# Layer 0 to 1 of a hybrid encoder: weight blocks split by VectorE, normed rows transposed one row tile later, one key transpose moved, no copy of group A's reciprocals

## The chip, the cores and the metric

The kernel runs on one core of a Trainium2 chip. The core has a matrix engine (TensorE, "PE" in the profile; its weight loads are "PEld"), three engines for elementwise work (VectorE "DVE", ScalarE "ACT", GpSimd "POOL"), SyncE ("SP"), which issues the DMAs, an on-chip memory (SBUF) and a small accumulator memory that PE writes (PSUM). Each engine has its own instruction queue and works it off in order; semaphores tie the queues together. The metric is the device time of one execution in microseconds (us). Lower is better.

## The reference: what is computed

Two encoder layers over a sequence of 1024 tokens with 1024 features, in float32. Each layer normalises x, projects it, runs two groups of attention heads beside each other, gates their outputs, projects the result, normalises it again and adds it to x:

```python
for l in range(DEPTH):                       # DEPTH = 2
    h = rms_norm(x, pre_norm_g[l])
    proj = h @ w_in[l]                       # 1024 x 3328
    aq, ak, av, ag, bq, bk, bv, bg = jnp.split(proj, SPLIT_POINTS, axis=-1)
    ...
    oa = diff_attention(...)                 # softmax(q1 k1) - lam * softmax(q2 k2), 4 heads
    oa = rms_norm(oa, diff_subln_g[l]) * (1.0 - lam_init)
    ya = oa.reshape(bn, s_len, A_WIDTH) * jax.nn.silu(ag)
    q = apply_rope(rms_norm(bq, q_norm_g[l]), cos, sin)   # 8 heads
    k = apply_rope(rms_norm(bk, k_norm_g[l]), cos, sin)   # 2 heads
    ob = gqa_attention(q, k, bv)
    yb = ob * jax.nn.silu(bg)
    y = jnp.concatenate([ya, yb], axis=-1) @ w_out[l]
    x = x + rms_norm(y, post_norm_g[l])
```

## The kernel before

**Precision.** Every float32 operand of a matmul is split into two parts in the format fp32r: a rounded one ("hi") and the rest ("lo"). ScalarE makes hi by a copy, and VectorE or GpSimd makes lo by a subtraction. A product is three matmuls (`mm3`: hi hi, hi lo, lo hi), so one row tile of 128 tokens by 512 columns is 8 x 3 = 24 matmuls (`mm_tok`).

**Tiling.** The tokens are 8 row tiles of 128. A projection goes through chunks of weight columns. `tok_chunk` runs over row tiles: 24 matmuls into PSUM, then a `post` function that hands the result on, then `follow`, which runs deferred steps whose due time ("beat", one per 512 columns) has come, then the `side` steps, mostly weight conversions. Every row tile of x must be transposed before it can be multiplied: `prenorm_b` transposes 8 blocks of 128x128 on PE into two PSUM tiles named pT (four blocks each), and `split` writes hi (ScalarE) and lo (VectorE) into the transposed tiles hT. PSUM holds **two** pT buffers in all; queries and keys use the same two.

**Weights.** `w_steps` gives the loads and the conversions of a chunk in blocks of 128x1024 elements. `on_dve` lists the blocks whose lo part VectorE makes; GpSimd makes the others.

**Layer 0, queries.** In the first stage the key/value columns are projected for the 8 tiles. Each tile's keys are scaled, and transposed some steps later (`bkv_store`: one transpose, split, four DMAs). The keys of tile 6 are transposed by the entry at due time 5 of the query chunk's `queue`, those of tile 7 at the same beat, and each tile's queries (`bq_store`: four transposes) two beats after they are made.

**Attention.** `all_items` yields score tiles for both groups, and `tick` lays the steps of several of them beside one another: scores, row sums, exponentials, transposes, product with V. For group A, `combine` forms reciprocals of the two row sums with VectorE; one scales the second softmax map, the other is copied into `r0`, from which `norm` and `gate` scale the result on GpSimd.

**Layer 0 to 1.** The output projection runs in two halves of 512 columns. In the second half's loop over row tiles t, the instructions of four engines keep the written order. For each t the loop does the residual of tile t-1 on VectorE (the result is x for the next layer and goes to DRAM), the norm of an earlier tile (`pre_normed`, VectorE), the transposes of a still earlier one (`pre_transposed`), the squares for the norm (`pre_scale`, ScalarE), then the 24 matmuls, the square and the scaling of their result (`out_half`), `post_scale`, and the `hooks` of that t: conversions of the next layer's key/value weights (`kv_convs`, two blocks) and query weights (`q_convs`, four blocks), the rotary tables, and the next layer's lambdas. The steps left over, `ends`, are run by layer 1: two at once, the others at the beats of `DUES`, between the key/value tiles (half a beat each).

The scale of a row goes through GpSimd: VectorE forms the mean square, GpSimd raises it to the power -1/2 (`rpow`).

Of the kernel before, what the change touches and what calls it, by code (L numbers as in the profile page):

```python
# [20 lines left out]
NT = 8  # L21
# [11 lines left out]
DVE_OUT = (1, 3)  # L33
ENDING = (1, 2, 3, 4, 0, 5)
BIAS = 3
DUES = (0.5, 1.5)
QSIDE = lambda c: {0: c[:1], 1: c[1:]}
FD = 1
OUTORD = True
# [12 lines left out]
def hybrid_encoder(ctx, tc, x, rel_bias, pre_norm_g, w_in, diff_lambda, diff_subln_g,  # L52
# [250 lines left out]
    def layer(l, hT, ends, given):  # L303
# [145 lines left out]
        if l == 0:  # L449
# [76 lines left out]
            queue.append((1, last_kv))  # L526
            for t in lates:
                queue.append((t - NT + LT, lates[t]))
            queue.append((5, lambda: lates[NT - 2]()))
            w_aq, loads, convs = w_steps(wl, C_AQ, on_dve=(1, 3))  # L530
            tok_chunk(w_q, bq_post, side={0: loads[:2], 1: convs[:1], 2: convs[1:2] + loads[2:], 4: convs[2:3],
                                          5: convs[3:]})
# [102 lines left out]
        def a_items(q, K, T5, t, qi, aT, r0, out):  # L635
            bias = T5[:, 896 - P * t:896 - P * t + 1024]
            es = [None, None]
            sums = s_tile(2, "asum", 4)
            items = []
            for c in range(2):  # L640
                def scores(c=c, box=[]):
                    pS = ps_s()
                    for i in range(2):
                        x0 = qi * 512 + i * 256 + c * P
                        for kh in range(2):
                            n = slice(kh * 512, kh * 512 + 512)
                            pe.matmul(pS[:, n], q[:, x0:x0 + P], K[:, c, n], start=(i == 0), stop=(i == 1))
                    return pS

                def reduce(pS, c=c):  # L650
                    es[c] = e_tile()
                    m = s_tile()
                    dve.tensor_tensor_reduce(out=es[c], in0=pS, in1=bias, op0=ALU.add, op1=ALU.min,
                                             scale=1.0, scalar=3.0e38, accum_out=m)
                    return m

                def expo(pS, m, c=c):
                    act.activation(es[c], es[c], AF.Exp, bias=m, scale=-1.0, accum_out=sums[:, c:c + 1])
                    if c == 1:
                        after(CD, combine)  # L660
                items.append((scores, reduce, expo))

            def combine():
                rec = s_tile(2, "arec", 4)
                dve.reciprocal(rec, sums)
                cc = s_tile()
                dve.scalar_tensor_tensor(cc, sums[:, 0:1], neglam, rec[:, 1:2], ALU.mult, ALU.mult)
                dve.tensor_copy(r0[:, qi:qi + 1], rec[:, 0:1])
                a, b = es
                gps.tensor_scalar(b, b, cc, 0.0, ALU.mult, ALU.add)  # L670
                gps.tensor_tensor(a, a, b, ALU.add)

                def go():
                    return transpose_unit(a, aT, qi, None) + [lambda: parts.extend(out or [])]
                trans.append((now[0] + AD, go))
            return items

        def a_out(h, g, aT, r0):
            box = []

            def part(i):
                if i == 0:
                    box.append(ps_o())
                pO = box[0][:, 0:256]
                V = values[h]
                for k in (2 * i, 2 * i + 1):
                    pe.matmul(pO, V[:, 0, k, :], aT[0][:, k, :], start=(k == 0), stop=False)
                    pe.matmul(pO, V[:, 0, k, :], aT[1][:, k, :], start=False, stop=False)
                    pe.matmul(pO, V[:, 1, k, :], aT[0][:, k, :], start=False, stop=(k == NK - 1))
                if i == 3:  # L690
                    after(0, lambda: finish(box[0]))

            def finish(pO):
                oT = o_tile((P, 256))
                act.copy(oT, pO[:, 0:256])
                p4 = pO[:, 256:512].rearrange("p (q c) -> p q c", c=P)
                ms = s_tile(2, "oms", 3)
                yv = [ys[g * 2 + qi][:, h * P:(h + 1) * P] for qi in range(2)]

                def norm():  # L700
                    for qi in range(2):
                        pe.transpose(p4[:, qi, :], oT[:, qi * P:(qi + 1) * P], ident)
                    for qi in range(2):
                        act.activation(oT[:, :P], p4[:, qi, :], AF.Square, accum_out=ms[:, qi:qi + 1])
                    after(1, gate, True)

                def gate():
                    for qi in range(2):
                        dve.tensor_tensor(yv[qi], p4[:, qi, :], yv[qi], ALU.mult)
                    fr = s_tile(2, "ofr", 3)  # L710
                    gps.tensor_tensor(fr, r0, r0, ALU.mult)
                    gps.tensor_tensor(ms, ms, fr, ALU.mult)
                    gps.tensor_scalar(ms, ms, 1.0 / P, EPS, ALU.mult, ALU.add)
                    gps.tensor_tensor(ms, ms, mhalf[:, :2], ALU.pow)
                    gps.tensor_tensor(fr, ms, r0, ALU.mult)
                    for qi in range(2):
                        gps.tensor_scalar(yv[qi], yv[qi], fr[:, qi:qi + 1], 0.0, ALU.mult, ALU.add)
                after(1, norm)

            return [lambda i=i: part(i) for i in range(4)]  # L720
# [105 lines left out]
        def all_items():  # L826
            for h in range(4):
                KA, T5 = state["ak"]
                if h:
                    load_av(h)  # L830
                if h == 0:
                    state["bv"] = h_tile([P, 2, NT, P], F32R)
                    nc.sync.dma_start(f(state["bv"]), bv_d)
                if h == 2:
                    state["bk"] = load_bk(1)
                BK, BV = state["bk"], state["bv"]
                for g in range(4):
                    q = state["q"]

                    if (h, g) != (3, 3):  # L840
                        state["q"] = load_q(h + (g + 1) // 4, (g + 1) % 4)
                    else:
                        for fn in half_loads:
                            fn()
                    if g == 0 and 0 < h < 3:
                        state["ak"] = load_ak(h + 1)
                    aT = new_probs()
                    bT = [None, None]
                    r0 = s_tile(2, "r0", 4)
                    sr = s_tile(4, "sr", 4)  # L850
                    a_parts = a_out(h, g, aT, r0)
                    b_parts = b_out(h, g, BV, bT, sr)
                    yield from a_items(q, KA, T5, g * 2, 0, aT, r0, None)
                    for j in range(2):
                        bT[j] = new_probs()
                        for qi in range(2):
                            if j and qi and not (h or g):
                                load_av(0)
                                state["ak"] = load_ak(1)
                            yield from b_items(q, BK, j, qi, bT, sr, b_parts[j] if qi else None)  # L860
                        if j == 0:
                            yield from a_items(q, KA, T5, g * 2 + 1, 1, aT, r0, a_parts)
# [106 lines left out]
        def pre_transposed(t):  # L969
            prenorm_b(t, yn[t], hN[t // 4])  # L970
# [8 lines left out]
        w = load_w(w_out[l], 512)  # L979
        hN, xts, hooks, nxt = [], [None] * NT, {}, None  # L980
        if not last:
            n_kv, kv_loads, kv_convs = w_steps(w_in[l + 1], C_BK, 256)
            n_q, q_loads, q_convs = w_steps(w_in[l + 1], C_BQ, on_dve=(3,))
            for fn in kv_loads + q_loads[:2]:
                fn()
            box = []
            hooks = {0: kv_convs[:1], 1: kv_convs[1:] + [lambda: box.extend(load_tables(l + 1))],
                     2: q_convs[:1] + [lambda: box.append(load_gains(l + 1))],
                     3: q_convs[1:2] + [lambda: box.append(lambdas(l + 1))],
                     4: [lambda: box.append(box[3]()), lambda: fill_tables(box[0], box[1], box[2], 1, gps)],  # L990
                     5: [lambda: fill_tables(box[0], box[1], box[2], 0, gps)], 7: q_loads[2:]}
        everything = [nc.tensor, nc.vector, nc.scalar, nc.gpsimd]
        for t in range(NT):
            xts[t] = e_tile()
# [2 lines left out]
            if t >= 1:  # L997
                residual(t - 1)
            if not last:
                if t in (3, 7):  # L1000
                    hN.append(new_h(t // 4))
                if t >= 2:
                    pre_normed(t - 2)
                if t >= 3:
                    pre_transposed(t - 3)
                if t >= 1:
                    pre_scale(t - 1)
            if last and t == NT - 1:
# [10 lines left out]
        else:  # L1019
            nxt = n_kv, n_q, q_convs[2:], box[0], *box[4]  # L1020

            def seventh():
# [1 line left out]
                residual(7)  # L1024
                pre_scale(7)

            ends = [lambda: pre_transposed(5), seventh, lambda: (pre_transposed(6), pre_normed(7))[:0],
                    lambda: pre_transposed(7)]
        inorder[:] = []
        return hN, nxt, ends  # L1030

# [57 lines left out]
```

## Time and profile before

| what | us |
|---|---|
| median of 3 runs | 1470.03 (1468.3 to 1470.81) |
| the profiled execution | 1470.85 |
| its span, first to last instruction | 1469.0 |
| PE busy | 1432.3 |
| VectorE busy | 843.9 |
| ScalarE busy | 775.3 |
| GpSimd busy | 741.7 |

The profile comes from one execution. Its span is the time from the first to the last instruction; the execution's own time is 1.85 us longer. Names of tiles are printed without their numbers: pS, pO and pT are PSUM tiles (scores and projections, projections and outputs, transposes), h are transposed rows, raw weights, keys and values, w converted weights and attention weights, y row tiles and their queries and keys, e temporaries of 128x1024, s small columns, o temporaries. In a timeline a row holds start, duration, engine, line, operation, output<-input, shapes and count; in brackets stands the engine's idle time ahead of it and who ended it. All instructions show line 65, because a helper class issues them, so one tells them apart by tiles and shapes.

### The profile page before, as it was taken

What the parts mean: (1) busy time and instruction counts of PE and PEld (TensorE: products, weight loads), DVE (VectorE), ACT (ScalarE), POOL (GpSimd) and SP (SyncE); (2) the same over time, 40 slices, a digit from 0 to 9 for tenths busy, and PEclk for the clock granted to TensorE, in tenths of its full rate; (3) what the DMA queues carried; (4) which work ended last, traced back from release to release, by engine and by line L of the source; (5) the groups of instructions that cost most, each with busy time, mean ns of one, the idle gap of its engine ahead of it and who ended that gap; (6) DMA issues with size and microseconds to landing.
All of it is one profiled execution on the core that took longest, in us unless ns stands there. A gap on an engine that the chain in (4) does not pass through costs nothing.

```text
span 1469.0 us, 22474 instructions
## 1 busy us (share of the span) xinstructions
PE 1432.3 (97%) x8300; PEld 1251.7 (85%) x8300; DVE 843.9 (57%) x1657; ACT 775.3 (53%) x1508; POOL 741.7 (50%) x743
## 2 busy tenths in 40 slices
PE   6999999999999999999899999999999999999998
PEld 6877888888999999988788888888799999998887
DVE  7851110038888888852786511100588888888424
ACT  5322122138888888852342322121588888888321
POOL 3541222018888888852433431120388888888320
PEclk9999999999999999999999999999999999999999
DMA  6468822165424322041335673223644142310303
GB/s 218 122 171 207 273 95 52 29 188 153 107 66 112 88 71 81 2 144 58 133 110 129 159 200 121 86 51 105 177 118 105 49 125 66 94 59 32 113 29 129
DMA packets 110669, 162.45 MB, mean 111 GB/s; under 512 B 8408, under 2 KB 72408, under 8 KB 108256
## 3 DMA queue, kind: packets, MB, share of 16 engines
q1 hardware_dynamic: 110560, 161.02, 37.8%
q8 instruction: 65, 1.06, 0.3%
q14 instruction: 44, 0.36, 0.1%
HBM read 112.72 MB, written 52.46 MB: 112 GB/s over the span
## 4 chain that ended last, share of the span: by engine, by line
PE 86%; issue 5%; DVE 4%; POOL 2%; ACT 1%; DMA 1%; POOLq 0%; SPq 0%; DVEq 0%; ACTq 0%
PE pS L65 39%; PE pO L65 34%; PE pT L65 12%; DVE y L65 2%; POOL w L65 1%; DVE h L65 1%; ACT e L65 1%; POOL e L65 0%; DVE s L65 0%; ACT w L65 0%; DMA y<-in_x_dram 0%; POOL s L65 0%; DVE w L65 0%; DMA h<-in_w_out_dram 0%; DVE e L65 0%
## 5 line engine op out<-in xcount | busy, mean ns | idle before, releaser
L65 PE MATMUL pO<-w,h 128*128 128x256 f32 (+1 forms) x3592 | 656.1, 331 | 0.2
L65 PEld LDWEIGHTS pO<-w,h 128*128 128x128 f32 x3592 | 569.5, 190 | 82.5 <-POOL w L65 0.8
L65 PE MATMUL pS<-h,h 128*128 128x512 f32 x1024 | 294.6, 409 | 0.0
L65 POOL TENSOR_TENSOR w<-h,w 128x1024 fp32r<-128x1024 f32 x56 | 135.3, 2435 | 267.2 <-ACT w L65 264.8
L65 PE MATMUL pT<-identr,e 128*128 128x128 f32 x1536 | 200.8, 273 | 1.5 <-DVE w L65 1.2
L65 PEld LDWEIGHTS pS<-h,h 128*128 128x128 f32 x1024 | 174.8, 189 | 24.6 <-ACT e L65 0.4
L65 PE MATMUL pS<-w,h 128*128 128x512 f32 (+1 forms) x912 | 195.4, 371 | 0.0
L65 POOL TENSOR_SCALAR e<-e,s 128x1024 f32<-128x1024 f32 x64 | 71.9, 1124 | 229.8 <-DVE s L65 229.8
L65 DVE TENSOR_TENSOR w<-pT,w 128x512 fp32r<-128x512 f32 x256 | 169.8, 684 | 31.6 <-ACT w L65 31.5
L65 PEld LDWEIGHTS pS<-w,h 128*128 128x128 f32 x912 | 159.7, 191 | 27.8
L65 PEld LDWEIGHTS pT<-identr,e 128*128 128x128 f32 x1536 | 172.6, 140 | 6.0 <-DVE w L65 5.1
L65 PE MATMUL pS<-h,w 128*128 128x512 f32 x768 | 177.0, 391 | 0.0
L65 POOL TENSOR_TENSOR s<-s,mhalf 128x2 f32<-128x2 f32 (+2 forms) x96 | 80.4, 838 | 189.9 <-DVE s L65 184.3
L65 POOL TENSOR_TENSOR w<-e,w 128x512 fp32r<-128x512 f32 x128 | 168.7, 1318 | 10.4
L65 PEld LDWEIGHTS pS<-h,w 128*128 128x128 f32 x768 | 143.4, 188 | 30.5 <-issue 0.5
L65 ACT CAST w<-pT 128x512 fp32r<-128x512 f32 x256 | 143.8, 588 | 45.8 <-PE pT L65 43.0
L65 DVE TENSOR_REDUCE s<-pS 128x1 f32<-128x1024 f32 x128 | 156.1, 1219 | 16.1 <-PE pS L65 15.2
L65 ACT ACTIVATE e<-e,s 128x1024 f32<-128x1024 f32 x128 | 148.1, 1157 | 22.4 <-DVE s L65 21.7
L65 DVE CUSTOM_DVE_ANT_0 e<-pS,h 128x1024 f32<-128x1024 f32 x128 | 155.4, 1215 | 5.5 <-PE pS L65 4.9
L65 POOL TENSOR_TENSOR e<-e,e 128x1024 f32<-128x1024 f32 x64 | 153.2, 2393 | 5.3
L65 ACT ACTIVATE e<-pS,s 128x1024 f32<-128x1024 f32 x128 | 144.5, 1129 | 7.3 <-issue 5.8
L65 ACT ACTIVATE o<-pO 128x128 f32<-128x128 f32 (+2 forms) x97 | 37.0, 382 | 130.6 <-PE pO L65 120.0
(77 smaller groups left out, 1095.6 us busy)
## 6 DMA issues: line engine op xcount, KB each, us to landing
h<-in_w_in_dram SPq DMA_DIRECT2D x52, 512.0 KB, 4.9
h<-aq_d SPq DMA_DIRECT2D x64, 256.0 KB, 5.1
bq_d<-y SPq DMA_DIRECT2D x64, 128.0 KB, 2.6
aq_d<-e SPq DMA_DIRECT2D x32, 256.0 KB, 4.4
ak_d<-e SPq DMA_DIRECT2D x16, 512.0 KB, 4.6
h<-bq_d SPq DMA_DIRECT2D x32, 256.0 KB, 6.0
h<-ak_d SPq DMA_DIRECT2D x16, 512.0 KB, 7.8
av_d<-e SPq DMA_DIRECT2D x32, 256.0 KB, 2.5
```

The lines of the kernel that those rows point to most:

```text
L65: ins = fn(*args, **kw)
```

## The change

It has four parts.

1. *Weight blocks.* Both key/value blocks of layer 1 and the first query block get their lo part from VectorE, not GpSimd. The second query block stays with GpSimd, but its conversion goes from the hooks of tile 3 to those of tile 6.
2. *Transposes.* In the second half's loop, the transposes of tile t-4 are issued at t (before: t-3), from t = 4 on. The second set of transposed tiles (rows 4 to 7) is created in `ends`, no longer at t = 7. `ends` has one step more, and `DUES` one beat more.
3. *Key transpose.* The entry for the keys of tile 6 in layer 0's query chunk goes from due time 5 to 4.
4. *Reciprocals.* `r0` has four columns. The reciprocals of both sums are written straight to it, with a stride of two, and the copy of 128x1 goes. The readers use its first two columns.

```diff
-DUES = (0.5, 1.5)
+DUES = (0.5, 1.0, 2.0)
...
-            queue.append((5, lambda: lates[NT - 2]()))
+            queue.append((4, lambda: lates[NT - 2]()))
...
             def combine():
-                rec = s_tile(2, "arec", 4)
+                rec = r0[:, qi::2]
                 dve.reciprocal(rec, sums)
                 cc = s_tile()
                 dve.scalar_tensor_tensor(cc, sums[:, 0:1], neglam, rec[:, 1:2], ALU.mult, ALU.mult)
-                dve.tensor_copy(r0[:, qi:qi + 1], rec[:, 0:1])
...
-                    gps.tensor_tensor(fr, r0, r0, ALU.mult)
+                    gps.tensor_tensor(fr, r0[:, :2], r0[:, :2], ALU.mult)
...
-                    gps.tensor_tensor(fr, ms, r0, ALU.mult)
+                    gps.tensor_tensor(fr, ms, r0[:, :2], ALU.mult)
...
-                    r0 = s_tile(2, "r0", 4)
+                    r0 = s_tile(4, "r0", 4)
...
-            n_kv, kv_loads, kv_convs = w_steps(w_in[l + 1], C_BK, 256)
-            n_q, q_loads, q_convs = w_steps(w_in[l + 1], C_BQ, on_dve=(3,))
+            n_kv, kv_loads, kv_convs = w_steps(w_in[l + 1], C_BK, 256, on_dve=(0, 1))
+            n_q, q_loads, q_convs = w_steps(w_in[l + 1], C_BQ, on_dve=(0, 3))
...
-                     3: q_convs[1:2] + [lambda: box.append(lambdas(l + 1))],
+                     3: [lambda: box.append(lambdas(l + 1))],
...
-                     5: [lambda: fill_tables(box[0], box[1], box[2], 0, gps)], 7: q_loads[2:]}
+                     5: [lambda: fill_tables(box[0], box[1], box[2], 0, gps)], 6: q_convs[1:2], 7: q_loads[2:]}
...
-                if t in (3, 7):
-                    hN.append(new_h(t // 4))
+                if t == 4:
+                    hN.append(new_h(0))
                 if t >= 2:
                     pre_normed(t - 2)
-                if t >= 3:
-                    pre_transposed(t - 3)
+                if t >= 4:
+                    pre_transposed(t - 4)
...
-            ends = [lambda: pre_transposed(5), seventh, lambda: (pre_transposed(6), pre_normed(7))[:0],
-                    lambda: pre_transposed(7)]
+            ends = [lambda: (hN.append(new_h(1)), pre_transposed(4)), seventh, lambda: pre_transposed(5),
+                    lambda: (pre_transposed(6), pre_normed(7))[:0], lambda: pre_transposed(7)]
```

On PE, in layer 0's query chunk, the order before (y_647 and y_714 are the keys of tiles 6 and 7, y_702 and y_766 queries of two tiles; of each group of 24 matmuls the first row is shown):

```order
L65 MATMUL pT_880<-identr,y_702 128x128 x4
L65 MATMUL pS_892<-w_324,h_84 128x512
...
L65 MATMUL pT_928<-identr,y_647 128x128
L65 MATMUL pT_937<-identr,y_714 128x128
L65 MATMUL pT_947<-identr,y_766 128x128 x4
L65 MATMUL pO_963<-w_324,h_84 128x512
```

And of the change:

```order
L65 MATMUL pT_879<-identr,y_647 128x128
L65 MATMUL pT_889<-identr,y_702 128x128 x4
L65 MATMUL pS_901<-w_324,h_84 128x512
...
L65 MATMUL pT_937<-identr,y_714 128x128
L65 MATMUL pT_947<-identr,y_766 128x128 x4
L65 MATMUL pO_963<-w_324,h_84 128x512
```

The transpose of tile 6's keys moved ahead of the earlier query group, so that each gap between matmul groups holds two pT tiles.

On VectorE, in the second half of layer 0's output projection, from the PSUM read of tile 0 to the norm of row 0, before (y_6920 and y_6965 are the rows of tiles 0 and 1, e_7234 and e_7273 their x, e_6878 the next layer's gain, s small scales):

```order
L65 TENSOR_TENSOR y_6920<-pO_7236,e_6876 128x512
L65 TENSOR_TENSOR s_7265<-s_6922,s_7262 128x1
L65 TENSOR_SCALAR s_7265<-s_7265 128x1
L65 SCALAR_TENSOR_TENSOR y_6920<-y_6920,s_7265,e_7234 128x1024
L65 TENSOR_SCALAR s_7279<-s_7277 128x1
L65 TENSOR_TENSOR y_6965<-pO_7282,e_6876 128x512
L65 TENSOR_TENSOR s_7311<-s_6967,s_7308 128x1
L65 TENSOR_SCALAR s_7311<-s_7311 128x1
L65 SCALAR_TENSOR_TENSOR y_6965<-y_6965,s_7311,e_7273 128x1024
L65 SCALAR_TENSOR_TENSOR y_6920<-y_6920,s_7279,e_6878 128x1024
```

And of the change (rows y_6856 and y_6901; w_7206 the lo part of the key/value weights):

```order
L65 TENSOR_TENSOR y_6856<-pO_7172,e_6812 128x512
L65 TENSOR_TENSOR s_7201<-s_6858,s_7198 128x1
L65 TENSOR_SCALAR s_7201<-s_7201 128x1
L65 TENSOR_TENSOR w_7206<-h_7164,w_7205 128x1024
L65 SCALAR_TENSOR_TENSOR y_6856<-y_6856,s_7201,e_7170 128x1024
L65 TENSOR_SCALAR s_7215<-s_7213 128x1
L65 TENSOR_TENSOR y_6901<-pO_7218,e_6812 128x512
L65 TENSOR_TENSOR s_7247<-s_6903,s_7244 128x1
L65 TENSOR_SCALAR s_7247<-s_7247 128x1
L65 TENSOR_TENSOR w_7206<-h_7164,w_7205 128x1024
L65 SCALAR_TENSOR_TENSOR y_6901<-y_6901,s_7247,e_7209 128x1024
L65 SCALAR_TENSOR_TENSOR y_6856<-y_6856,s_7215,e_6814 128x1024
```

The two subtractions of the key/value weights now stand between the small scales of a tile and its residual; on GpSimd they are gone.

On PE, from tile 2 of that half on, before (the first row of each matmul group; y_6920, y_6965 are rows 0 and 1):

```order
L65 MATMUL pO_7330<-w_7212,h_6880 128x512
...
L65 MATMUL pT_7382<-identr,y_6920 128x128 x4
L65 MATMUL pT_7389<-identr,y_6920 128x128 x4
L65 MATMUL pO_7401<-w_7212,h_6925 128x512
...
L65 MATMUL pT_7443<-identr,y_6965 128x128 x4
L65 MATMUL pT_7450<-identr,y_6965 128x128 x4
L65 MATMUL pO_7462<-w_7212,h_6970 128x512
```

And of the change (y_6856, y_6901 are rows 0 and 1):

```order
L65 MATMUL pO_7266<-w_7148,h_6816 128x512
...
L65 MATMUL pO_7319<-w_7148,h_6861 128x512
...
L65 MATMUL pT_7363<-identr,y_6856 128x128 x4
L65 MATMUL pT_7370<-identr,y_6856 128x128 x4
L65 MATMUL pO_7382<-w_7148,h_6906 128x512
...
L65 MATMUL pT_7435<-identr,y_6901 128x128 x4
L65 MATMUL pT_7442<-identr,y_6901 128x128 x4
```

Tile 3's matmuls now stand between those of tile 2 and the transposes of row 0, and all later transposes follow one tile later: row 4 stands ahead of the first key/value tile of layer 1, row 5 behind the first, row 6 behind the second and row 7 behind the fourth. Before, row 5 stood ahead of the first, row 6 behind the first and row 7 behind the third.

## The prediction

> **What bounds the kernel now.** I read the busy time by stage first, then the TensorE (PE) timeline around each place where PE was not busy, then the engine that it waited for.
>
> ```profile
> span 1469.0 us, 22474 instructions
> 136.00:312.00 176.00, 176.00 (x777) 145.80 (x777) 21.31 (x23) 33.32 (x43) 28.90 (x12) 1.00 0.43 136
> 340.00:627.00 287.00, 286.96 (x2028) 265.76 (x2027) 250.82 (x507) 251.52 (x507) 239.83 (x272) 1.00 0.30 80
> 690.00:766.00 76.00, 69.64 (x360) 58.16 (x359) 54.59 (x85) 29.26 (x60) 28.40 (x27) 0.96 0.35 122
> ```
>
> The columns are the stretch, its length, then busy time of PE, PE's weight loads, VectorE (DVE), ScalarE (ACT) and GpSimd (POOL), PE's granted clock, DMA share and GB/s. In layer 0's later projections (136 to 312) PE is busy all the time, in its attention (340 to 627) 286.96 of 287.00 us: nothing off PE can be worth time there. The stage between the layers (690 to 766) has 6.4 us without a matmul and a clock of 0.96. So only places where PE waits matter. The change touches two of them.
>
> The first is in layer 0's query chunk:
>
> ```profile
> 70.82 0.60 PE L65 MATMUL pT<-identr,y 128*128 128x128 f32 x4
> 71.18 5.74 PE L65 MATMUL pS<-w,h 128*128 128x512 f32 x24
> 76.75 0.38 PE L65 MATMUL pT<-identr,y 128*128 128x128 f32 x2
> 80.58 0.66 PE L65 MATMUL pT<-identr,y 128*128 128x128 f32 x4 [3.45 <-DVE y L65]
> 80.99 7.31 PE L65 MATMUL pO<-w,h 128*128 128x512 f32 x24
> 88.14 0.60 PE L65 MATMUL pT<-identr,y 128*128 128x128 f32 x4
> ```
>
> Two key transposes (tiles 6 and 7) run at 76.75, and the query tile's four behind them wait 3.45 us for VectorE. Only two pT buffers exist: the third transpose group needs the first one's buffer back. VectorE gives it back late:
>
> ```profile
> 74.31 0.68 DVE L65 TENSOR_TENSOR y<-pT,y 128x512 fp32r<-128x512 f32 x1
> 80.24 0.48 DVE L65 TENSOR_TENSOR y<-pT,y 128x128 fp32r<-128x128 f32 x2
> ```
>
> The split of both key tiles runs at 80.24, behind a whole query tile's rotary work. PE goes on 0.3 us later, and its next 24 matmuls take 7.31 us instead of 5.74.
>
> The second place is the end of layer 0's output projection:
>
> ```profile
> 677.97 32.90 PE L65 MATMUL pO<-w,h 128*128 128x512 f32 x144
> 713.98 1.94 PE L65 MATMUL pT<-identr,y 128*128 128x128 f32 x8 [3.11 <-DVE y L65]
> 715.57 7.80 PE L65 MATMUL pO<-w,h 128*128 128x512 f32 x24
> ...
> 738.84 1.25 PE L65 MATMUL pT<-identr,y 128*128 128x128 f32 x8 [1.04 <-DVE h L65]
> 739.85 5.75 PE L65 MATMUL pO<-w,h 128*128 128x512 f32 x24
> 746.16 1.26 PE L65 MATMUL pT<-identr,y 128*128 128x128 f32 x8 [0.56 <-DVE h L65]
> ...
> 757.17 1.06 PE L65 MATMUL pT<-identr,y 128*128 128x128 f32 x8 [0.55 <-DVE y L65]
> 757.99 3.11 PE L65 MATMUL pO<-w,h 128*128 128x256 f32 x24
> 760.94 3.04 PE L65 MATMUL pS<-w,h 128*128 128x256 f32 x24
> 763.85 1.06 PE L65 MATMUL pT<-identr,y 128*128 128x128 f32 x8
> 764.67 3.12 PE L65 MATMUL pO<-w,h 128*128 128x256 f32 x24
> 767.63 2.68 PE L65 MATMUL pS<-w,h 128*128 128x512 f32 x11
> ```
>
> Six row tiles end at 710.87 (713.98 less 3.11), so a tile takes 5.45. From start to start a key/value tile takes 2.94 and eight transposes 0.8. From 710.87 to the first query matmul at 767.63 PE has to do five tiles (27.25), eight groups of transposes (6.4) and four key/value tiles (11.75): 45.4 us. It took 56.8. **11.4 us** are waits and slow matmuls (7.80 against 5.75), and no more can be won there.
>
> **The change, part by part.**
>
> *Key transpose of tile 6 one query tile earlier.* It now stands at 70.82, in front of the query's four. The row at 70.82 shows no wait, so a buffer is free there, and the other was split a turn earlier. The groups then run as key 6, query, key 7, query, and the second pair takes the buffers of the first, whose splits VectorE does at about 74.3 to 75.1 (the row at 74.31, with the key's 0.2 ahead of it). At 76.75 neither group waits. PE does the same transposes (0.11 us each), so the matmuls of 80.99 start at 77.3 and, without a wait ahead of them, take 5.6 to the next transposes: 82.9 instead of 88.14, **5.3 us less**. The bounds are 0 (the wait comes back elsewhere) and 5.3. On SP the key's four stores go ahead of three query stores. What stands behind them, the next weight loads, is paced by conversions that move with PE. With PE busy 176.00 of 176.00 us in the stretch that follows, nothing there gives the time back; I take all of 5.3.
>
> *Blocks converted by VectorE.* Three GpSimd subtractions of 128x1024 (two key/value blocks, one query block) become VectorE's, and one query block's goes from after tile 3 to after tile 6.
>
> ```profile
> 700.67 1.04 ACT L65 CAST w<-h 128x1024 fp32r<-128x1024 f32 x1
> 700.81 0.69 DVE L65 TENSOR_TENSOR y<-pO,e 128x512 f32<-128x512 f32 x1 [4.69 <-ACT o L65]
> 702.35 2.40 POOL L65 TENSOR_TENSOR w<-h,w 128x1024 fp32r<-128x1024 f32 x1
> 702.42 3.42 DVE L65 SCALAR_TENSOR_TENSOR y<-y,s,e 128x1024 f32<-128x1024 f32 x1 [0.67 <-POOL s L65]
> 709.24 4.59 DVE L65 SCALAR_TENSOR_TENSOR y<-y,s,e 128x1024 f32<-128x1024 f32 x2 [0.67 <-POOL s L65]
> 735.71 2.47 DVE L65 SCALAR_TENSOR_TENSOR y<-y,s,e 128x1024 f32<-128x1024 f32 x2
> 766.52 1.21 DVE L65 TENSOR_TENSOR w<-h,w 128x1024 fp32r<-128x1024 f32 x1
> ```
>
> VectorE's residual took 3.42 while GpSimd's 2.40 ran, two of its kind 4.59 beside another, and 2.47 (1.2 each) undisturbed: a GpSimd block costs VectorE about 2.1 us. Done by VectorE it costs 1.21. So each moved block shortens VectorE's queue by 0.9 us, although a conversion now stands ahead of the residual: residual 0 ends at 701.7 (ACT's cast) + 1.2 + 1.2 = 704.2 instead of 705.8, and the normed row 0 is there by about 711.5 instead of 713.8. What queues behind the conversion on VectorE are the residual, ScalarE's square of it and the next PSUM read. All end earlier than before.
>
> *Transposes one row tile later.* Tile 3's matmuls now fill the 3.11 us: they run from 710.87 to 716.3, row 0 has been ready for nearly 5 us, and the slow clock behind the wait has no cause. Next late is VectorE's split of each transposed tile, which gives the two pT buffers back:
>
> ```profile
> 731.58 0.67 DVE L65 TENSOR_TENSOR y<-pO,e 128x512 f32<-128x512 f32 x1
> 740.96 4.54 DVE L65 SCALAR_TENSOR_TENSOR y<-y,s,e 128x1024 f32<-128x1024 f32 x2 [0.66 <-POOL s L65]
> 755.75 2.47 DVE L65 SCALAR_TENSOR_TENSOR y<-y,s,e 128x1024 f32<-128x1024 f32 x2
> 761.23 1.29 DVE L65 TENSOR_TENSOR h<-pT,h 128x512 fp32r<-128x512 f32 x2 [0.20 <-ACT h L65]
> ```
>
> 1. Tile 4 ends at 717.1 + 5.45 = 722.55, transposes of row 1 follow with 0.1 wait at most, tile 5 ends at 728.85.
> 2. Behind tile 4, VectorE has the next layer's lambdas. From its PSUM read (731.58) to the transposes that need the split at that iteration's end (738.84) it took 7.26. Now the read starts 0.8 after tile 4 (as 700.81 after 700.0), at 723.35, so row 2 is transposed at 730.6: **1.75 wait**. Tile 6 runs from 731.6 to 737.05.
> 3. The next turn of VectorE, with table filling on GpSimd beside it (4.54 for two), took 7.32 (738.84 to 746.16). Row 3 comes at 738.0: **0.95 wait**; tile 7 ends at 744.5.
> 4. The late query block on GpSimd makes the following turn as long: row 4 at 745.3, **0.8 wait**. The block's buffer becomes part of the second h tile; read to the end at about 743 (begun at 740.3, 2.40 long), it is needed at 746.
> 5. Row 5 comes between the first two key/value tiles without a wait (749.3). Row 6 needs row 5's split. Its chain held 755.75 + 2.47 to 761.23 + 0.65, or 3.65; the residual of tile 7 now ends at about 750.8 (row 3's split to 746.0, the PSUM read and two scales 1.1, row 4's split 1.3, two long ones 2.47), so row 6 is transposed at 754.4 where PE is ready at 753.0: **1.35 wait**.
> 6. Row 7 follows two key/value tiles later without a wait. Four waits lengthen their transposes by 0.2 each (1.25 against 1.03 to 1.06).
>
> Sum: 45.4 + 4.85 + 0.8 + 0.1 = 51.2 instead of 56.8, **5.6 us less**. Bounds: 0 and 11.4. I take 5.6, nearest to the rows with the same sequence of VectorE work.
>
> *No copy of the reciprocals.*
>
> ```profile
> L65 DVE COPY s<-s 128x1 f32<-128x1 f32 x64 | 9.4, 147 | 0.0
> ```
>
> 64 VectorE copies of 147 ns go, 9.4 us. The reciprocal writes the same two columns with a stride. They lie beside PE's 286.96 of 287: I take 0 (bounds 0 and -9.4, the latter if all stood on PE's path).
>
> **The clock.** The new waits are 0.8 to 1.75 us. Do they slow the matmuls behind them, as 3.45 and 3.11 did?
>
> ```profile
> 31.20 1.25 PE L65 MATMUL pT<-identr,y 128*128 128x128 f32 x8 [1.74 <-DVE h L65]
> 32.21 3.12 PE L65 MATMUL pS<-w,h 128*128 128x256 f32 x24
> 714.00:717.40 3.40, 3.40 (x12) 3.04 (x13) 2.48 (x7) 2.40 (x5) 2.50 (x3) 0.50 0.73 246
> 717.40:720.80 3.40, 3.40 (x11) 2.67 (x10) 3.40 (x3) 1.15 (x2) 0.94 (x1) 0.61 0.18 69
> ```
>
> Behind the wait of 3.11 the granted clock was 0.50 and then 0.61 for 6.8 us. Behind 1.74 the 24 matmuls took 3.12, as long as behind none (764.67). So I count no slow clock. [...]
>
> **Rivals.**
>
> - *The wait only moves at the stage between the layers.* VectorE is busy 54.59 of 76 there, and if its turns are longer than I walked, 11.4 stay lost: 1470.85 - 5.3 = 1465.6. Against it: VectorE's list gets shorter by 3 x 0.9. 0.10.
> - *The key edit does not free the buffer* (the query group still finds a taken one): 1470.85 - 5.6 = 1465.3. Against it is the row at 74.31. 0.05.
> - *The short waits vanish as well*, because VectorE, never behind, starts each turn earlier: up to 1470.85 - 5.3 - 11.4 = 1454.2. 0.08.
> - *Slower: the clock falls at each short wait.* Four waits stand 4 to 9 us apart, and one fall lasted 6.8 us, so the clock would be down from 730 to 756. PE's 19.7 us of work there (two tiles, three key/value tiles) at 0.555 become 35.5: +15.8, 1475.9. It decides from the point where a wait under 1.8 us trips the clock; 31.20 speaks against it. [...] 0.03.
>
> **How the numbers follow.** The profiled execution took 1470.85 (span 1469.0), 0.8 above the median 1470.03. Its time less 5.3 and 5.6 is 1459.95: I predict **1460.0**. The forecast has 0.70; another 0.04 goes to a loss that I don't see, which eats most of the gain. The range 1456 to 1466 takes in the first two rivals and an error of 4 us downward, and leaves out the fourth and most of the third. A measurement of this kernel tells about 0.2% (2.9 us) from no change. The first three rivals and the forecast are faster by more than that: 0.91 with a little taken off; within it 0.06; slower 0.03.
>
> **What would show it.** Right: no wait ahead of the transposes near 77, matmuls of 5.7 behind them, and layer 0's later stages 5.3 earlier; no wait of 3 us near 705, clock 1.00 in that stage, residuals of 1.2 for tiles 0 to 2; waits for VectorE's h of 1 to 2 us ahead of rows 2, 3, 4 and 6, the longest behind the lambdas; attention as long as before. Wrong: a wait of over 2.5 us anywhere in that stage, or a granted clock below 0.95 behind a short one; a weight load that lands late because its buffer came free late.

## The result, and the profile after

| kernel | median us | lowest to highest | runs |
|---|---|---|---|
| before | 1469.99 | 1468.3 to 1470.81 | 6 |
| the change | 1459.94 | 1459.78 to 1460.1 | 6 |

The ratio is 0.9932 (95% interval 0.992 to 0.9945): 10.05 us less, where 1460.0 us was predicted. The profiled execution of the change took 1459.86 us (span 1457.8), 10.99 less than that of before. Its runs also agree more closely than those of before, which becomes important below.

The PE timeline of the changed kernel in layer 0's query chunk:

```profile
70.91 0.71 PE L65 MATMUL pT<-identr,y 128*128 128x128 f32 x5
71.37 5.75 PE L65 MATMUL pS<-w,h 128*128 128x512 f32 x24
76.96 0.71 PE L65 MATMUL pT<-identr,y 128*128 128x128 f32 x5
77.43 5.75 PE L65 MATMUL pO<-w,h 128*128 128x512 f32 x24
83.02 0.60 PE L65 MATMUL pT<-identr,y 128*128 128x128 f32 x4
```

Key and query transposes stand together (x5). The 3.45 us wait is gone, the 24 matmuls take 5.75 instead of 7.31, and the next transposes start at 83.02 instead of 88.14: 5.12 us. VectorE splits the key and its query group one after the other (one row, named by the key's shape), before the next pair needs the buffers:

```profile
74.40 0.88 DVE L65 TENSOR_TENSOR y<-pT,y 128x128 fp32r<-128x128 f32 x2
```

The PE timeline between the layers:

```profile
672.86 38.34 PE L65 MATMUL pO<-w,h 128*128 128x512 f32 x168
711.04 1.03 PE L65 MATMUL pT<-identr,y 128*128 128x128 f32 x8
...
717.49 1.25 PE L65 MATMUL pT<-identr,y 128*128 128x128 f32 x8
718.50 5.70 PE L65 MATMUL pO<-w,h 128*128 128x512 f32 x24
725.62 1.26 PE L65 MATMUL pT<-identr,y 128*128 128x128 f32 x8 [1.42 <-DVE h L65]
...
732.92 1.26 PE L65 MATMUL pT<-identr,y 128*128 128x128 f32 x8 [0.60 <-DVE h L65]
...
740.31 1.25 PE L65 MATMUL pT<-identr,y 128*128 128x128 f32 x8 [0.64 <-DVE h L65]
...
749.04 1.25 PE L65 MATMUL pT<-identr,y 128*128 128x128 f32 x8 [0.86 <-DVE h L65]
...
756.68 5.74 PE L65 MATMUL pS<-w,h 128*128 128x512 f32 x24
```

Seven tiles now run through. Row 0 is transposed without a wait, and waits of 1.42, 0.60, 0.64 and 0.86 us remain at rows 2, 3, 4 and 6, all for VectorE's split of an earlier row. Row 1 waits a little too. PE's row at 717.49 doesn't show it, but those of its weight loads (PEld) do, ahead of the first four transposes and of the second four:

```profile
717.49 0.42 PEld L65 LDWEIGHTS pT<-identr,y 128*128 128x128 f32 x4 [0.39 <-DVE h L65]
718.09 0.42 PEld L65 LDWEIGHTS pT<-identr,y 128*128 128x128 f32 x4 [0.18 <-DVE s L65]
```

This is also why eight transposes take 1.25 there and not 1.03: the second four wait for VectorE in the middle of the group. From the start of the row tiles to the first query matmul the stage takes 83.82 us (672.86 to 756.68); before it took 89.66 (677.97 to 767.63). That is 5.84 us, the other half of the gain.

Two stretches of the changed kernel, with the columns of the table in the prediction, show the attention of layer 0 and the stage between the layers:

```profile
335.00:622.00 287.00, 286.96 (x2028) 265.96 (x2028) 249.21 (x478) 250.56 (x507) 239.61 (x272) 1.00 0.30 80
690.00:756.00 66.00, 62.48 (x344) 52.57 (x343) 52.64 (x91) 28.66 (x60) 23.95 (x24) 1.00 0.38 126
```

PE's busy time in the attention is the same 286.96, although VectorE has 29 instructions fewer. In the stage the granted clock is 1.00, where it was 0.96.

VectorE, then GpSimd, in the first turns of that stage:

```profile
696.63 1.23 DVE L65 TENSOR_TENSOR w<-h,w 128x1024 fp32r<-128x1024 f32 x1
698.30 1.28 DVE L65 SCALAR_TENSOR_TENSOR y<-y,s,e 128x1024 f32<-128x1024 f32 x1 [0.45 <-POOL s L65]
703.99 2.48 DVE L65 SCALAR_TENSOR_TENSOR y<-y,s,e 128x1024 f32<-128x1024 f32 x2 [0.44 <-POOL s L65]
...
696.72 1.55 POOL L65 TENSOR_TENSOR s<-s,mhalf 128x1 f32<-128x1 f32 x1 [11.62 <-DVE s L65]
701.04 0.56 POOL L65 TENSOR_TENSOR s<-s,mhalf 128x1 f32<-128x1 f32 x1 [2.77 <-DVE s L65]
```

VectorE converts a block in 1.23, and its residuals take 1.28, and 2.48 for two, instead of 3.42 and 4.59. New is the row at 696.72: GpSimd's power of a single column, 0.56 elsewhere, takes 1.55 beside the conversion, so the residual behind it starts 0.45 late.

### The profile page after: what moved, and what is told of

Read it like the earlier page. It is cut to its first block, busy times and chain, and to the rows that moved or that the text cites. A ratio compares the mean times of both kernels' runs of the same rounds, so it can differ in the third digit from the quotient of the medians.

```text
span 1457.8 us, 22409 instructions
## 1 busy us (share of the span) xinstructions
PE 1427.4 (98%) x8300; PEld 1248.3 (86%) x8300; DVE 838.0 (57%) x1596; ACT 773.4 (53%) x1508; POOL 736.1 (50%) x740
## 4 chain that ended last, share of the span: by engine, by line
PE 91%; DVE 4%; ACT 2%; issue 1%; POOL 1%; DMA 0%; POOLq 0%; DVEq 0%; SPq 0%; ACTq 0%
PE pS L65 40%; PE pO L65 39%; PE pT L65 13%; DVE y L65 2%; DVE h L65 1%; ACT w L65 1%; ACT e L65 1%; POOL e L65 0%; DVE s L65 0%; DVE w L65 0%; DMA e<-in_pre_norm_g_dram 0%; ACT h L65 0%; POOL w L65 0%; ACT o L65 0%; POOL s L65 0%
## 5 line engine op out<-in xcount | busy, mean ns | idle before, releaser
L65 POOL TENSOR_TENSOR w<-h,w 128x1024 fp32r<-128x1024 f32 x53 | 127.2, 2421 | 266.8 <-ACT w L65 266.8
```

The source lines that it names most:

```text
L65: ins = fn(*args, **kw)
```

## The experiments

**Parts alone.** Each of four runs makes one part of the change in the kernel before, whose median beside them was 1469.97 us (28 runs, 1468.42 to 1472.25).

*Key transpose alone:*

```diff
-            queue.append((5, lambda: lates[NT - 2]()))
+            queue.append((4, lambda: lates[NT - 2]()))
```

> The kernel before with the key edit alone (tile 6's key transpose one query tile earlier). My theory: the 3.45 us wait ahead of the query transposes at 80.58 and the slow 24 matmuls behind it go, 5.1 to 5.3 us, and nothing later gives them back: about 1464.8 us. The rival, that the wait only moves to the next group of transposes: within 2 us of the kernel before.

Measured: 1464.5 us (5 runs, 1464.35 to 1465.86), ratio 0.9966 (0.9954 to 0.9978), 5.5 less. The wait does not come back elsewhere; the rival falls.

*VectorE's blocks alone:*

```diff
-            n_kv, kv_loads, kv_convs = w_steps(w_in[l + 1], C_BK, 256)
-            n_q, q_loads, q_convs = w_steps(w_in[l + 1], C_BQ, on_dve=(3,))
+            n_kv, kv_loads, kv_convs = w_steps(w_in[l + 1], C_BK, 256, on_dve=(0, 1))
+            n_q, q_loads, q_convs = w_steps(w_in[l + 1], C_BQ, on_dve=(0, 3))
```

> The kernel before with VectorE's weight blocks alone (two key/value blocks and the first query block converted by VectorE; transposes as before, behind tile t-3, the second query block still on GpSimd in iteration 3). By the changed kernel's rows row 0 is normed some 4.6 us earlier than its transposes could be in the kernel before less 2.3, so the wait of 3.11 shrinks to about 0.7, the clock stays up, and waits of about 1.2, 1.5 and 0.9 us come at the later rows: 5.3 us less, about 1464.7 us, so that the blocks alone would bring nearly all of what the stage between the layers gave. Rival, that it takes the later transposes to remove the wait (the blocks save 0.9 of VectorE's queue each, which leaves a wait of over 2 us with the slow clock behind it): 1 to 2 us less, about 1468.5.

Measured: 1466.43 us (10 runs, 1465.59 to 1467.39), ratio 0.9978 (0.9969 to 0.9987), 3.5 less, between the two. Its PE timeline sides with the theory:

```profile
713.02 1.06 PE L65 MATMUL pT<-identr,y 128*128 128x128 f32 x8 [0.86 <-DVE y L65]
713.84 5.74 PE L65 MATMUL pO<-w,h 128*128 128x512 f32 x24
```

The wait of 3.11 is down to 0.86 with nothing moved, and the matmuls behind it run at 5.74. The stage takes 84.62 us, 5.0 less than before. Why the whole kernel gained less than its stage is answered with the clock below.

*Later transposes alone* (t-4 instead of t-3, with `ends`, `DUES` and the second query block as in the change; blocks on GpSimd as before):

```diff
-                if t >= 3:
-                    pre_transposed(t - 3)
+                if t >= 4:
+                    pre_transposed(t - 4)
```

> The kernel before with the later transposes alone (each row one tile later, the second query block behind tile 6, blocks converted by GpSimd as before). My walk: row 0 no longer waits, but VectorE is behind by the long residuals beside GpSimd's blocks, and a wait of about 2.9 us comes at row 1, then 1.5, 0.8, 0.9 and 1.35. If that wait leaves the clock up: 2.8 us less, about 1467.2. If a wait of 2.9 us slows the clock as the one of 3.11 did: no gain, about 1470. Rival, that moving the transposes is what brings the gain and the blocks add nothing: 5.8 less, about 1464.2.

Measured: 1470.06 us (10 runs, 1468.86 to 1470.3), ratio 0.9999 (0.9989 to 1.0008): nothing. PE, and below it VectorE's long operations of the turn in question:

```profile
716.21 1.03 PE L65 MATMUL pT<-identr,y 128*128 128x128 f32 x8
...
726.02 1.33 PE L65 MATMUL pT<-identr,y 128*128 128x128 f32 x8 [3.32 <-DVE h L65]
727.03 7.33 PE L65 MATMUL pO<-w,h 128*128 128x512 f32 x24
...
716.10 4.58 DVE L65 SCALAR_TENSOR_TENSOR y<-y,s,e 128x1024 f32<-128x1024 f32 x2 [0.46 <-POOL s L65]
```

Row 0 no longer waits, but row 1 waits 3.32 us and the clock falls behind it (0.52 granted over 727.2 to 730.6). Row 0's split, whose pT buffers row 1 needs, stands behind residuals that GpSimd's blocks (4.58 for two) have held up. The wait has changed its row and nothing else. The profiled execution (1468.9) is one of the faster ones; its stage takes 87.66 us, 2.0 less than in the profile of before, but no less than the stage of before where the clock stays up (87.30, shown below).

*No copies, alone* (the edit of `combine` and `r0` from the diff of the change):

> The kernel before without the 64 copies of group A's reciprocals (the reciprocal writes them into place). My theory: nothing, within 0.7 us of the kernel before, since they lie beside a TensorE that is busy 286.96 of 287 us in the attention. Rival, that they stand on TensorE's path: up to 9.4 us less.

Measured: 1469.49 us (11 runs), ratio 0.9995 (0.9986 to 1.0004). No effect, as expected.

**The change without its later transposes:**

> The changed kernel with the transposes put back one row tile earlier (behind tile t-3, second query block on GpSimd in iteration 3); key edit, VectorE's blocks and the copies stay. From the start of the row tiles to the first query matmul the blocks alone took 84.62 us, the whole change 83.82: 0.8 more than the changed kernel, about 1460.7 us. Rival, that moving the transposes is worth nothing once the blocks are VectorE's (alone it gave 0): 1459.9. Rival, that it is worth half of the stage's 5.8: 1462.8.

Measured: 1461.4 us (4 runs, 1460.62 to 1462.19); the profiled execution took 1460.66, with a stage of 84.57 us. With the change's 83.82 beside it, moving the transposes is worth 0.75 us once the blocks are VectorE's. It was worth nothing before that. The medians differ by 1.46 because two of the four runs are 1.5 us slower than the other two; what slows them isn't shown, as neither was profiled.

**What the remaining waits consist of.** The next three runs change the changed kernel further. First, the lambdas are computed in layer 1's projections:

```diff
-                     3: [lambda: box.append(lambdas(l + 1))],
-                     4: [lambda: box.append(box[3]()), lambda: fill_tables(box[0], box[1], box[2], 1, gps)],
+                     4: [lambda: fill_tables(box[0], box[1], box[2], 1, gps)],
...
+        if l:
+            lam = lambdas(l)
         col_chunk(w_aq, -0.125, store_q)
+        if l:
+            gsub, neglam = lam()
```

> The changed kernel with the next layer's lambdas computed in layer 1's projections instead of between the row tiles. The wait ahead of row 2's transposes (1.42 us) was put down to the lambdas. My theory: they go, but GpSimd's table filling, which ran beside them, now runs beside VectorE's two long operations (4.54 instead of 2.47, as in the turn behind), so a wait of 0.6 stays: 0.8 less than the changed kernel, about 1459.1 us. Rival, that the lambdas were all of it: 1.6 less (the wait and 0.2 of its transposes), 1458.3. Rival, that the turn is as long for another reason: 1459.9.

Measured: 1460.85 us (4 runs, three of 1460.83 to 1460.87 and one of 1459.42). The stage takes 83.43 us, 0.39 less than in the change. PE at row 2, and VectorE's turn ahead of it:

```profile
726.59 1.25 PE L65 MATMUL pT<-identr,y 128*128 128x128 f32 x8 [0.98 <-DVE h L65]
...
721.41 4.53 DVE L65 SCALAR_TENSOR_TENSOR y<-y,s,e 128x1024 f32<-128x1024 f32 x2 [0.73 <-POOL s L65]
```

The lambdas are gone, and the two long operations take 4.53 instead of 2.47 beside GpSimd's filling (1.28 at 721.34, 2.27 at 722.58), which has found something else to hold up. So the theory was right in kind and half right in size: a wait of 0.98 stays where 0.6 had been expected, and the stage gives 0.39 and not 0.8. The median is even 0.9 above the change's; the profiled execution is one of the three slower runs, and what slows it lies elsewhere, shown with the clock below.

Second, the fillings and the second query block go to VectorE, and the lambdas stay where the change has them:

```diff
-            n_q, q_loads, q_convs = w_steps(w_in[l + 1], C_BQ, on_dve=(0, 3))
+            n_q, q_loads, q_convs = w_steps(w_in[l + 1], C_BQ, on_dve=(0, 1, 3))
...
-                     4: [lambda: box.append(box[3]()), lambda: fill_tables(box[0], box[1], box[2], 1, gps)],
-                     5: [lambda: fill_tables(box[0], box[1], box[2], 0, gps)], 6: q_convs[1:2], 7: q_loads[2:]}
+                     4: [lambda: box.append(box[3]()), lambda: fill_tables(box[0], box[1], box[2], 1, dve)],
+                     5: [lambda: fill_tables(box[0], box[1], box[2], 0, dve)], 6: q_convs[1:2], 7: q_loads[2:]}
```

> The changed kernel with the last GpSimd operations of the stage between the layers done by VectorE: both table fillings (two operations of 128x512 each, about 0.7 us each by the row of that shape) and the second query block (1.22). If a GpSimd operation always costs VectorE more than doing it itself: three turns shorter by 0.3 to 0.9, so 0.5 to 1.5 us less than the changed kernel, 1458.4 to 1459.4. My theory: the first filling costs VectorE little now, since it lies beside the lambdas and not beside the long operations, so it adds 1.1 to row 2's wait, against 0.25 and 0.45 less at rows 3 and 4: 0.4 more, about 1460.3 us.

Measured: 1458.25 us (4 runs, 1458.23 to 1458.34), 1.7 less than the change. My theory fell: it had 0.4 more. PE at rows 2 and 3, then VectorE at the end of the lambdas:

```profile
725.23 1.25 PE L65 MATMUL pT<-identr,y 128*128 128x128 f32 x8 [0.99 <-DVE h L65]
...
731.83 1.03 PE L65 MATMUL pT<-identr,y 128*128 128x128 f32 x8
...
720.76 0.22 DVE L65 TENSOR_SCALAR gsub<-gsub 128x128 f32<-128x128 f32 x1
```

and the same place in the change, VectorE and then GpSimd:

```profile
720.46 0.80 DVE L65 TENSOR_TENSOR neglam<-s 128x1 f32<-128x1 f32 x1 [0.27 <-ACT s L65]
721.36 1.21 DVE L65 TENSOR_SCALAR gsub<-gsub 128x128 f32<-128x128 f32 x1
...
719.95 1.29 POOL L65 TENSOR_TENSOR h<-h,ng 128x512 f32<-128x512 f32 x1
721.20 1.28 POOL L65 TENSOR_TENSOR h<-h,ngs 128x512 f32<-128x512 f32 x1
```

I had read the filling as hidden beside the lambdas. It was not: the scaling of gsub takes 0.22 us by itself and 1.21 beside the filling, as long as one filling operation, and the row of neglam falls from 0.80 to 0.16. That is 1.6 us saved against 1.2 for the two fillings on VectorE, so row 2's wait went down as well, by 0.43 (from 1.42 to 0.99), where I had added 1.1.

Third, both together:

> Late lambdas and all of the stage on VectorE together. My theory: every turn of VectorE is then 2.5 of long operations plus 1.2 to 1.4 of own conversion or filling plus 0.45 for GpSimd's stretched power, about 7.0 or below against TensorE's 6.45, so the waits ahead of rows 2, 3 and 4 come down to 0.2 to 0.4 each, row 6's stays 0.9: about 1.8 to 2.2 us less than the changed kernel, 1458.0 us. Rival, that they do not add up (the stretched power eats what the filling saves): as late lambdas alone, 1459.1.

Measured: 1456.9 us (4 runs, 1456.83 to 1458.24), ratio to before 0.9918 (0.9901 to 0.9934), 3.0 less than the change and the fastest version here. Its stage takes 80.80 us. PE at rows 2, 3, 4 and 6:

```profile
724.12 1.03 PE L65 MATMUL pT<-identr,y 128*128 128x128 f32 x8
...
730.46 1.10 PE L65 MATMUL pT<-identr,y 128*128 128x128 f32 x8
...
737.18 1.25 PE L65 MATMUL pT<-identr,y 128*128 128x128 f32 x8
...
746.08 1.26 PE L65 MATMUL pT<-identr,y 128*128 128x128 f32 x8 [1.02 <-DVE h L65]
```

Of the waits shown on PE three are gone and one is left, so the gain is larger than the 1.8 to 2.2 of the theory, which had left 0.2 to 0.4 at each of the three; the rival, that the two don't add up, falls. A last version tied the lambdas behind layer 1's last query tile, to take them out of the way of row 6:

> Late lambdas and all of the stage on VectorE, with the lambdas tied behind layer 1's last query tile. In the version before this one the scheduler had put their four small operations (0.9 us) on VectorE at 742.3, ahead of the split of row 5 that row 6's transposes waited for (1.02 us). If these are what that wait consists of: it falls to about 0.2, 0.8 to 1.0 less, about 1456.0 us. Rival, that row 6 waits for the two long operations ahead of them (2.47, at 739.9): 1456.9 as without this edit.

Measured: 1458.27 us (5 runs, 1456.87 to 1458.38); the profiled execution took 1456.87, with a stage of 80.82. The median is in the slower of two groups of times that the clock section below explains as far as the runs do; the profile tells the cause. Row 6 still waits 0.97, so the lambdas were not it: where they stood, VectorE now waits 1.22 us for ScalarE (743.52). Nor are the two long operations the last link: ScalarE, then VectorE, ahead of that row:

```profile
742.34 1.06 ACT L65 ACTIVATE e<-y 128x1024 f32<-128x1024 f32 x1 [3.24 <-DVE y L65]
...
744.46 0.27 ACT L65 CAST e<-pS 128x128 fp32r<-128x128 f32 x1 [0.81 <-DVE e L65]
744.62 1.08 ACT L65 CAST h<-pT 128x512 fp32r<-128x512 f32 x2
...
743.52 0.15 DVE L65 TENSOR_SCALAR s<-s 128x1 f32<-128x1 f32 x1 [1.22 <-ACT e L65]
...
745.25 1.29 DVE L65 TENSOR_TENSOR h<-pT,h 128x512 fp32r<-128x512 f32 x2 [0.20 <-ACT h L65]
```

VectorE's split of row 5 waits for ScalarE's cast of the same row, which stands behind a cast of key/value tile 0 that itself waits 0.81 us for VectorE. VectorE in turn had waited for ScalarE's squares (742.34), and these for the two long operations, so the rival names the start of the chain. The order of these two casts on ScalarE would be the next thing to change; it was not tried.

**Is it the wait that lowers the clock?** The kernel before with the key edit gets 12 matmuls ahead of row 0's transposes, whose result nobody reads:

```diff
+                if t == 3:
+                    filler = ps_s((P, 512))
+                    for i in range(FILLER):
+                        pe.matmul(filler, yTs[3][0][:, i % NK, :], w[0][i % NK], start=(i == 0), stop=(i == FILLER - 1))
                 if t >= 3:
                     pre_transposed(t - 3)
```

> The kernel before with the key edit, and 12 matmuls of 128x512 ahead of row 0's transposes in the stage between the layers; nobody reads their result. They take 2.7 us of the wait of 3.11 there and move nothing else. If the idle time is what lowers the clock: no slow matmuls behind it, 24 matmuls in 5.74 instead of 7.34 and transposes in 1.03 instead of 1.16, so up to 1.7 us below the key edit's median (1464.5), about 1462.8 us, though TensorE does more. Rival, that the clock falls there for another reason (the load of the engines beside it): 1464.5 as without them.

Measured: 1464.87 us (5 runs: 1463.21 and 1463.3, and three of 1464.87 to 1464.97). The ratio to before is 0.9966, that of the key edit alone, so in the median the added matmuls gain nothing, as the rival had it. The profiled execution (1463.21) is one of the two faster ones. The key edit alone, then with the 12 matmuls:

```profile
708.98 1.16 PE L65 MATMUL pT<-identr,y 128*128 128x128 f32 x8 [3.11 <-DVE y L65]
709.80 7.34 PE L65 MATMUL pO<-w,h 128*128 128x512 f32 x24
...
705.50 2.88 PE L66 MATMUL pS<-w,h 128*128 128x512 f32 x12
708.78 1.06 PE L66 MATMUL pT<-identr,y 128*128 128x128 f32 x8 [0.40 <-DVE y L66]
709.60 5.72 PE L66 MATMUL pO<-w,h 128*128 128x512 f32 x24
```

With PE kept busy the matmuls take 5.72 (clock 1.00 over 708.8 to 712.2), where the key edit's took 7.34 behind a wait of 3.11. (The added lines of code make its line number 66.) The stage takes 87.33 instead of 88.49, 1.16 less; the rest of the 1.6 went into longer waits behind it. This fits the theory that the idle time lowers the clock, but one execution doesn't show it, because a wait of that length doesn't always lower it. The kernel without copies, whose stage is that of before:

```profile
714.12 1.06 PE L65 MATMUL pT<-identr,y 128*128 128x128 f32 x8 [3.08 <-DVE y L65]
714.94 5.73 PE L65 MATMUL pO<-w,h 128*128 128x512 f32 x24
```

A wait of 3.08, and no slow matmuls: this stage takes 87.30. The wait of 3.45 at 80.6 was followed by slow matmuls in all four profiles that have it (7.16 to 8.10). And short waits sometimes are. In the first stage, which no run here touches, PE waits 1.74 us at 31.2 and, where nothing happens there, 1.8 at 41.1. VectorE's blocks alone at the first place, late lambdas at the second:

```profile
31.29 1.69 PE L65 MATMUL pT<-identr,y 128*128 128x128 f32 x8 [1.74 <-DVE h L65]
32.62 4.33 PE L65 MATMUL pS<-w,h 128*128 128x256 f32 x24
...
41.04 0.33 PE L65 MATMUL pT<-identr,y 128*128 128x128 f32 x1 [1.81 <-DVE h L65]
...
43.26 3.85 PE L65 MATMUL pS<-w,h 128*128 128x256 f32 x24
```

In the profile of before the same matmuls took 3.12 and 3.11. The granted clock is 0.61 over 31.2 to 34.6 in the first of these executions, and 0.52 over 41.4 to 44.8 in the second. A fall at 32 costs nothing, since the wait at 41 shrinks to about 0.5 (best_ordered's profile has 4.61 at 32.23 and a wait of 0.49 at 41.07). A fall at 41 puts all that follows later: the row tiles start at 674.25 in the profile with late lambdas and at 672.86 in that of the change. These 1.4 us are also what lies between the two groups of times in the runs with late lambdas, and the runs of several other versions (best_ordered, key_filled, VectorE's blocks alone) fall into two groups 1.4 to 1.7 apart. Their slower group doesn't always come from this place. VectorE's blocks alone were profiled in theirs (1467.03), and there it is the fall behind the 3.45 us wait in the query chunk that was longer than in the profile of before (7.31), with a granted clock of 0.50 and 0.59 over 80.4 to 87.2, where before had 0.70 and 0.80:

```profile
81.46 8.10 PE L65 MATMUL pO<-w,h 128*128 128x512 f32 x24
```

This answers most of why VectorE's blocks alone gained 3.5 us and not the 5.0 of their stage. In these two profiles the row tiles start at 679.25 with the blocks and at 677.97 before, so that 1.28 of the 5.0 was lost ahead of the stage, by the longer fall. And the profiled execution of before lies 0.9 above its median; it had the fall behind its 3.11 us wait (matmuls of 7.80), which the profile without copies does not have (5.73). Against the stage without that fall (87.30) the blocks' 84.62 is 2.7 less.

## Why the prediction was right, point by point

- *Key transpose, 5.3:* 5.12 in the two profiles, 5.5 between the medians of the run with this part alone. Right, and by the mechanism: key 6 and its query group are split at 74.4, before the next pair needs the buffers.
- *Blocks on VectorE:* a residual beside no GpSimd block took 1.28, near the 1.2 assumed. The residual of tile 0 ended at 699.58, in the frame of before (5.12 later) 704.70; 704.2 was predicted. The 0.5 is the stretched power, which the prediction had not seen. Row 0 was normed at 711.6 in that frame, against 711.5.
- *Transposes one tile later, 5.6 for the stage:* the profiles give 5.84. Waits were predicted at rows 2, 3, 4 and 6, the longest behind the lambdas, which held, with 1.75, 0.95, 0.8 and 1.35. They measured 1.42, 0.60, 0.64 and 0.86, so three of the four are below the 1 to 2 us that the text gave as its sign. Most of the difference is where the count begins. The profile counts a wait from the end of a group's last matmul, 5.70 after the group's start (718.50 to 724.20 ahead of row 2); the walk counted from 5.45 after it, the distance of two groups with nothing between them. Counted as in the walk, the four waits are 1.67, 0.84, 0.92 and 1.03. Where VectorE arrived was right: row 2 is transposed at 725.62, predicted 730.6 less 5.12, or 725.5. What the walk lacked is VectorE's split of row 0 at row 1, which costs PE 0.3 us (its start 0.1 late, its transposes 0.2 longer) where at most 0.1 was counted. From the sixth tile's end (672.86 and 32.90, or 705.76) to the first query matmul it is 50.9 us, against 51.2. Two slips in the sums change nothing: 32.90 for six tiles is 5.48 each and not 5.45, and the slow rival's time is 1475.8.
- *Which edit does it:* the text let tile 3's matmuls fill the 3.11 us. The runs show the blocks doing most of it: alone they leave 0.86 of that wait, while the later transposes alone move it whole to row 1. Added to the blocks, the later transposes are worth 0.75. Most of the gain is VectorE's shorter queue, and PE's new order adds to it only when that queue is short.
- *The clock:* no slow matmuls behind the new waits, and the granted clock is 1.00 in the stage, as predicted. The rule behind it was too simple, though. The prediction took 3.11 as enough and 1.74 as too short; the runs show 3.08 without a fall and 1.74 with one. So the 11.4 us that the prediction found to be won included about 2.4 that only some executions pay: with no fall the stage of before takes 87.3, not 89.66, and the change wins 3.5 there, not 5.84. The medians lie between: from the key edit alone (1464.5) to the whole change (1459.94) it is 4.6. The total came out at 1459.94 because the profiled execution of the change has no slow matmuls behind its waits at 31, at 41 and in the stage, and its other runs are as fast; the prediction had started from an execution of before that had some. That it met the median to 0.1 us is luck: two parts were off by 0.2 in opposite directions.
- *Copies, 0:* confirmed by itself.
- *The rivals:* a wait that only moves is what the later transposes alone show (3.32 at row 1), so that rival was real, and the blocks are why it did not come true. The short waits don't vanish by themselves, but do when GpSimd's last operations and the lambdas leave the stage (3.0 us less).

## What to carry to other kernels

Where TensorE waits for VectorE, look first at what GpSimd does beside VectorE's long operations: here a GpSimd operation cost VectorE nearly its own length (2.1 of 2.40 us), so doing it on VectorE itself (1.2) made VectorE's queue shorter. Moving a waiting step back paid here only once the queue it waits for was short enough (0.75 us with the blocks on VectorE, nothing without them); otherwise the wait changed its row (3.32 at row 1), so measure such parts singly. Price a TensorE wait as a band, with and without the slow clock behind it (89.66 and 87.30 us for the stage here), since one profiled execution shows only one of the two.

## What the hardware showed that was not expected

- Holding-up between GpSimd and VectorE went both ways: a GpSimd power on one column rose from 0.56 to 1.55 beside VectorE's 1.23 conversion, and VectorE's scaling of 128x128 from 0.22 to 1.21 beside a GpSimd operation of 1.28. In both pairs of rows the held-up operation ended after the other one, the power 0.41 us later (698.27 and 697.86) and the scaling 0.09 us later (722.57 and 722.48).
- Behind nearly the same wait on TensorE the matmuls were sometimes slow, at a lower granted clock, and sometimes not. In the stage between the layers 24 of them took 7.80 us behind 3.11 (clock 0.50, then 0.61) and 5.73 behind 3.08 in the kernel without copies. Behind 1.74 at 31.2 they took 3.12 in the profile of before (1.00 over 31.2 to 34.6) and 4.33 with VectorE's blocks alone (0.61). What decides in a single execution isn't settled here.
